# Compression of cached blocks beside dense products: one batch of 64 products a half block in place of two of 32, second layer behind the batch, five turned tiles

## The chip, the core and the metric

One core of a Trainium2 chip runs the whole program. The metric is the device time of one execution in microseconds; the time before is the median of three runs, 1340.01 us (1339.94 to 1341.91). The engines are named as in the profile: PE (TensorE, matmul; PEld its weight loads), DVE (VectorE), ACT (ScalarE), POOL (GpSimd) and SP (SyncE, which here only issues DMAs). Each engine takes its instructions in order; waits between engines go over semaphores.

## The reference

One inference step of a two-layer decoder: 256 prompt tokens and 8 x 4 sample tokens, 288 in all, width 1024. Layer 0 mixes with a gated short convolution, layer 1 with native sparse attention; each has a half-step SwiGLU FFN (2816 wide) before and after it. What the change touches is the compressed branch of the sample rows: blocks of 32 cached rows, gathered over a page table, go through a two-layer MLP into one key and one value.

```python
def compress(rows, pe, w1k, w2k, w1v, w2v):
    B, T = rows.shape[:2]
    blk = rows.reshape(B, T // L_CMP, L_CMP, 2, N_KV_HEADS, HEAD_DIM) + pe[:, None, None, :]
    k = jax.nn.gelu(jnp.einsum('bnlkd,lde->bnke', blk[:, :, :, 0], w1k)) @ w2k
    v = jax.nn.gelu(jnp.einsum('bnlkd,lde->bnke', blk[:, :, :, 1], w1v)) @ w2v
    return k, v
...
past_c = cache_cmp[page_table].reshape(B, past, 2, N_KV_HEADS, HEAD_DIM)
```

The past blocks hang on the cache alone, not on the tokens, so they can be compressed at any time before attention.

## The kernel before

**Dense work.** Weights are streamed by SP into four buffers of 8 KB a partition (`raw`, L96). `Weights.convert` splits each *unit* of at most 8 x 128 x 128 into an exact pair: `whi` by ACT (L116), `wlo` = weight minus `whi` by DVE (L117; a few by POOL). A product (`product`, L177 for every matmul) is three matmuls for each k: hi x hi, hi x lo, lo x hi, all 288 tokens wide. So an up unit of 8 k has 24 matmuls, a down unit of the first half of the hidden values 18 (six k), of the second half 15 (five k). Taking a unit first splits ahead, up to two units beyond the one taken (`AHEAD = 2`).

**Phases.** Three FFNs run with the compression beside them: the first and second around the conv mixer of layer 0, the third ahead of attention. An FFN has for values f0 to f11 two products each (gate, up), then a down phase over d0 to d7 with two units each (a, b), then f12 to f21 and a second down phase. After a pair of products `evacuate` (L484 to L494) takes them over: DVE scales the gate (t), ACT applies Silu (s), DVE scales the other, POOL multiplies (a), and one step later ACT and DVE make the pair Ah, Al of it, the inputs of the down products. In the second down phase each d also updates the residual xT (L523), and `gated` makes from it xh (ACT), xl (DVE), a square (ACT) and adds it up (POOL). At d4 a tiny Sqrt (`root`, L527) brings ACT's table for Sqrt ahead of the norm's own Sqrt (`rms`, L352), which comes after the next phase's first products. Silu and Tanh come from other tables than Sqrt. The conv mixer has 24 products in, three for each d, with gates and taps (L541 to L569), and eight products out.

**Side work.** `cmp_side` (from L713) is a Python generator that the planner resumes: after each unit `tick(cost)` runs what was put off (`later`), then adds cost x FILL (0.13) to what is owed, and steps the generator until the shares it yields have used that up. A tick costs 3.0 in an up phase and in the mixer, 2.2 in a down phase. The place of side work in every engine's queue is therefore fixed by the order of the program.

**Compression.** There are 64 gathered tiles (`load`, L733: a POOL indirect DMA of 512 KB into four slots `rc`). Each is turned by DVE (`turn`, L739) into one of three slots `rt`, and turning tile i starts the gather of tile i + 4. Four tiles make one half block (b, h). Each tile is the moving operand of eight matmuls, which stand as 16 products in the profile (`acc<-rt,W`, two passes each), so a half has 64. Before, they come as two batches of 32 with a pause of 2.0 behind each. `gelu_hidden` (L696 to L699: ACT Hx and its square, DVE, POOL) and `gelu_hidden2` (L703 to L705: Tanh on ACT, DVE, POOL) make the hidden values; `second` (the products `acc<-Hs,W` and `acc<-W,Hs`, then DVE's copy KcT, L791, and ACT's copy Vc, L792) is the second layer, run in the half that follows, behind the pause after its first batch. Ahead of the loop POOL multiplies W1 with the positions (L750) and DVE reduces that (L754) for the bias b1.

Of the kernel before, what the change touches and what calls it, by code (L numbers as in the profile page):

```python
# [10 lines left out]
F32 = mybir.dt.float32  # L11
# [7 lines left out]
P = 128  # L19
D = 1024  # L20
# [17 lines left out]
# buffers: loaded weights, split weights, gathered pages  # L38
RAW, SPLIT, PAGES = 4, 4, 5
ATT = dict(mm=3, tr=3, acc=2)  # L40

# the start: which tile of the input DVE squares, products that warm the array up, steps from a part's
# split to its products, when the tokens' factors are wanted, where weights are split and by which engine
# [4 lines left out]
# the past blocks' compression beside the dense products: its share of the time, and what its loads take  # L48
# [3 lines left out]
# attention: the order of the steps of a round (see nsa), the prompt's items a step, how many of them are  # L52
# kept for the last rounds, where the small steps of a pair of sequences go, which turns ACT takes, and
# where the output projection's weights are split
# [11 lines left out]
class Weights:  # L66
    """The weight stream: chunks of at most 8 KB a partition are loaded ahead, each is split into an
    exact pair of float32r parts, unit by unit, ahead of its products."""
# [76 lines left out]
def tile_step(ctx, tc, x_prompt, x_sample, state_conv, cache_cmp, cache_sel, cache_win, page_table,  # L145
# [33 lines left out]
    # ---- inputs wanted first  # L179
# [3 lines left out]
    xv = [ffn0.tile([P, D], F32, name="rt", bufs=3) for a in range(3)]  # L183
# [24 lines left out]
    # ---- constants  # L208
# [14 lines left out]
    # ---- the stream of weights  # L223
# [78 lines left out]
    # ---- the residual stream, transposed: [d, token]  # L302
# [39 lines left out]
    def gated(d, v):  # L342
        """The normed input's part without the token's factor, as an exact pair; the squares' sum."""
        gated_hi(d, v)
        gated_lo(d, v)
        squares(d)
# [10 lines left out]
    def begin(pg, pu):  # L357
        """The first products, each step as soon as its part of the input has been turned and split."""
        nc.scalar.activation(root, eps, AF.Sqrt)
        r = tmp.tile([P, 4], F32, name="rn")  # L360
        for a in range(3):
            m = min(P, N - a * P)
            sq = ffn0.tile([P, D], F32, name=f"sq{a % 2}", bufs=1)
# [4 lines left out]
        warm = accb()  # L368
# [56 lines left out]
    def products2(p0, p1, ah, al, late=2, between=None):  # L425
        """Two outputs at a phase's start: the inputs that come last are used last."""
# [15 lines left out]
    def tick(cost):  # L442
        """After each unit of dense work: what was put off, and a share of the side work."""
# [165 lines left out]
    # ---- the last norm: turned as it comes, scaled when the tokens' factors are known  # L609
# [45 lines left out]
    # ---- the compressed branch's past blocks: they hang on the cache alone  # L655
# [8 lines left out]
    def indices():  # L664
        # a gathered row is two tokens of a block: partition (q, n) takes tokens 8 q + 2 i of block n
# [47 lines left out]
    def cmp_side(cw):  # L713
# [4 lines left out]
        # rows (q, d) and steps (i, l, h) of a block's token 8 q + 2 i + l and column 32 h + d  # L718
# [17 lines left out]
        def turn(i):  # L736
            if i < 64:
                turned[i] = cw.tile([P, 1024], F32, name="rt", bufs=3)
                nc.vector.transpose(turned[i], tiles.pop(i))  # L739
                load(i + 4)  # L740
# [4 lines left out]
        turn(0)  # L745
        # the first layer's share of the positions: a product with one column
        part = []
        for h in range(2):
            t = cw.tile([P, 1024], F32, name="rt", bufs=3).rearrange("p (s e) -> p s e", s=8)
# [11 lines left out]
        turn(1)  # L761
        second = None
        for b in range(NB):
            for h in range(2):
                H = accb()
                for j in range(4):
                    i = b * 8 + h * 4 + j
                    v = turned.pop(i).rearrange("p (l c k h n) -> p c l h k n", l=2, c=2, k=KV, h=2)
                    turn(i + 2)
                    for st in range(4):  # L770
# [3 lines left out]
                        if st == 3 and j % 2:  # L774
                            yield 2.0
                    if j == 0 and second:
                        gelu_hidden2(*hidden)
                    if j == 1 and second:
                        second()
                        yield 0.6  # L780
# [13 lines left out]
        yield 0.5  # L794
        gelu_hidden2(*hidden)
        yield 1.0
# [734 lines left out]
```

## Time and profile before

| | |
|---|---|
| median of three runs | 1340.01 us |
| span of the profiled execution | 1333.6 us |
| DVE busy, ACT busy, POOL busy | 815.4, 616.7, 353.5 us |
| compression products on PE, first to last | 106.0 to 771.0 us |
| gathers of the compression | 64, median 5.2 us to landing |
| transposes | 64, 78.3 us of DVE |
| granted clock of PE | 0.995 |

The profile shows one execution. Its rows of groups give line, engine, operation, names, shapes and count, then busy time and mean duration in ns, then idle time ahead of them with what ended it. Rows of the timeline give start, duration, engine, line, operation, names and count, and in brackets the idle time ahead and what ended it. Rows of windows give the stretch in us, its length, the busy time of PE with its count, the granted clock, the DMA share and GB/s. Rows of waits give the waiting group, the group that ended the wait, the total, the count and the longest. Matmuls overlap, so a matmul's duration (about 300 ns) is longer than the step from one start to the next (132 ns), and PE counts as busy in gaps shorter than that; starts are what to read.

### The profile page before, as it was taken

What the parts mean: (1) busy time and instruction counts of PE and PEld (TensorE: products, weight loads), DVE (VectorE), ACT (ScalarE), POOL (GpSimd) and SP (SyncE); (2) the same over time, 40 slices, a digit from 0 to 9 for tenths busy, and PEclk for the clock granted to TensorE, in tenths of its full rate; (3) what the DMA queues carried; (4) which work ended last, traced back from release to release, by engine and by line L of the source; (5) the groups of instructions that cost most, each with busy time, mean ns of one, the idle gap of its engine ahead of it and who ended that gap; (6) DMA issues with size and microseconds to landing.
All of it is one profiled execution on the core that took longest, in us unless ns stands there. A gap on an engine that the chain in (4) does not pass through costs nothing.

```text
span 1333.6 us, 26864 instructions
## 1 busy us (share of the span) xinstructions
PE 1309.6 (98%) x11009; PEld 1242.0 (93%) x11009; DVE 815.4 (61%) x1512; ACT 616.7 (46%) x1115; POOL 353.5 (27%) x356
## 2 busy tenths in 40 slices
PE   8999999999999999999999999999999999999997
PEld 8999999999999999999999999998776688999997
DVE  5675566677666555667655555666556456554553
ACT  5443444443454433345433445454766655443444
POOL 2331233243323222333321121303333123220211
PEclk9999999999999999999999999999999998999999
DMA  8767555756565575457656344765577964766432
GB/s 261 197 195 245 187 189 171 234 183 204 191 194 192 162 236 198 144 181 246 193 171 206 127 143 144 215 192 222 206 269 285 300 165 163 246 251 221 142 118 75
DMA packets 202893, 262.12 MB, mean 197 GB/s; under 512 B 14958, under 2 KB 188610, under 8 KB 197524
## 3 DMA queue, kind: packets, MB, share of 16 engines
q1 hardware_dynamic: 179792, 182.34, 43.5%
q0 software_dynamic: 14304, 75.61, 16.0%
q10 hardware_dynamic: 8676, 2.48, 1.0%
q8 instruction: 86, 1.41, 0.4%
q14 instruction: 35, 0.29, 0.1%
HBM read 257.38 MB, written 11.35 MB: 202 GB/s over the span
## 4 chain that ended last, share of the span: by engine, by line
PE 87%; DVE 6%; ACT 4%; issue 2%; POOL 1%; DMA 0%; ACTq 0%; SPq 0%; POOLq 0%; DVEq 0%
PE mm L177 74%; PE acc L177 8%; PE tr L221 4%; DVE wlo L117 2%; ACT whi L116 1%; DVE rt L739 1%; DMA rt<-in_x_prompt_dram 0%; ACT sq L332 0%; ACT wlo L1166 0%; ACT S L1166 0%; DVE xT L523 0%; ACT L527 0%; ACT whi L1280 0%; DVE xl L326 0%; POOL ue L542 0%
## 5 line engine op out<-in xcount | busy, mean ns | idle before, releaser
L177 PE MATMUL mm<-xh,whi 128*128 128x288 f32 x1832 | 548.5, 299 | 2.2 <-DVE xl L1215 0.9
L177 PE MATMUL mm<-xh,wlo 128*128 128x288 f32 x1832 | 544.1, 297 | 2.7 <-DVE wlo L117 1.7
L177 PE MATMUL mm<-xl,whi 128*128 128x288 f32 x1832 | 536.7, 293 | 1.1 <-DVE xl L326 1.1
L117 DVE TENSOR_TENSOR wlo<-raw,whi 128x1024 fp32r<-128x1024 f32 (+2 forms) x358 | 402.2, 1136 | 109.0 <-ACT whi L116 107.2
L116 ACT ACTIVATE whi<-raw 128x1024 fp32r<-128x1024 f32 (+2 forms) x365 | 343.1, 953 | 107.8 <-PE mm L177 90.7
L177 PEld LDWEIGHTS mm<-xh,whi 128*128 128x128 f32 x1832 | 344.8, 188 | 8.1 <-issue 3.9
L177 PEld LDWEIGHTS mm<-xl,whi 128*128 128x128 f32 x1832 | 349.1, 191 | 2.8 <-DVE xl L326 2.5
L177 PEld LDWEIGHTS mm<-xh,wlo 128*128 128x128 f32 x1832 | 344.2, 188 | 3.7 <-DVE wlo L117 2.4
L490 POOL TENSOR_TENSOR a<-s,t 128x288 f32<-128x288 f32 x88 | 111.9, 1271 | 445.8 <-DVE t L488 273.0
L177 PE MATMUL mm<-Ah,whi 128*128 128x288 f32 x768 | 229.4, 299 | 0.0
L177 PE MATMUL mm<-Ah,wlo 128*128 128x288 f32 x768 | 227.9, 297 | 0.7 <-DVE wlo L117 0.7
L177 PE MATMUL mm<-Al,whi 128*128 128x288 f32 x768 | 227.5, 296 | 0.0
L177 PEld LDWEIGHTS mm<-Ah,whi 128*128 128x128 f32 x768 | 145.2, 189 | 2.6 <-issue 1.9
L177 PEld LDWEIGHTS mm<-Ah,wlo 128*128 128x128 f32 x768 | 144.1, 188 | 1.4 <-DVE wlo L117 1.4
L177 PEld LDWEIGHTS mm<-Al,whi 128*128 128x128 f32 x768 | 144.4, 188 | 0.0
L486 ACT ACTIVATE s<-t 128x288 f32<-128x288 f32 x88 | 39.1, 445 | 172.4 <-DVE t L484 170.4
L733 POOL DMA_INDIRECT rc<-in_cache_cmp_kv_dram,idxc x64 | 70.8, 1107 | 134.2 <-DVE rt L739 117.0
L493 ACT ACTIVATE Ah<-a 128x288 fp32r<-128x288 f32 x88 | 39.2, 445 | 128.0 <-POOL a L490 127.7
L488 DVE TENSOR_TENSOR t<-mm,rB 128x288 f32<-128x288 f32 x88 | 39.9, 454 | 79.1 <-PE mm L177 79.1
L739 DVE STREAM_TRANSPOSE rt<-rc 128x1024 f32<-128x1024 f32 x64 | 78.3, 1233 | 9.2 <-PE acc L177 9.1
L494 DVE TENSOR_TENSOR Al<-a,Ah 128x288 fp32r<-128x288 f32 x88 | 40.0, 454 | 58.8 <-ACT Ah L493 58.8
L523 DVE SCALAR_TENSOR_TENSOR xT<-mm,xT 128x288 f32<-128x288 f32 x64 | 29.2, 456 | 71.2 <-PE mm L177 70.9
(348 smaller groups left out, 1249.3 us busy)
## 6 DMA issues: line engine op xcount, KB each, us to landing
raw<-in_w_ffb_gu_dram SPq DMA_DIRECT2D x44, 1024.0 KB
raw<-in_w_ffa_gu_dram SPq DMA_DIRECT2D x42, 1024.0 KB
raw<-in_w_ffa_down_dram SPq DMA_DIRECT2D x16, 768.0 KB
raw<-in_w_conv_in_dram SPq DMA_DIRECT2D x12, 1024.0 KB
raw<-in_w_ffb_down_dram SPq DMA_DIRECT2D x16, 768.0 KB
raw<-in_w_ffa_down_dram SPq DMA_DIRECT2D x16, 640.0 KB
raw<-in_w_ffb_down_dram SPq DMA_DIRECT2D x16, 640.0 KB
out_dram<-in_cache_win_kv_dram POOLq DMA_DIRECT2D x8, 1016.0 KB, 6.9
```

Source lines behind the costliest of these rows:

```text
L116: self.nc.scalar.activation(parts[0], v, AF.Copy)
L117: (lower or self.nc.vector).tensor_sub(parts[1], v, parts[0])
L177: nc.tensor.matmul(out, lhsT, rhs, start=start, stop=stop, skip_group_check=True)
L221: nc.tensor.transpose(out, in_, ident[:k, :k])
L486: nc.scalar.activation(s1, t1, AF.Silu)
L488: nc.vector.tensor_mul(t2, pu[:, :N], rB)
L490: nc.gpsimd.tensor_mul(a, s1, t2)
L493: nc.scalar.activation(Ah[:, f], a, AF.Copy)
L494: nc.vector.tensor_sub(Al[:, f], a, Ah[:, f])
L523: nc.vector.scalar_tensor_tensor(xT[:, d], py[:, :N], 0.5, xT[:, d], op0=OP.mult, op1=OP.add)
L733: nc.gpsimd.indirect_dma_start(out=tiles[i], out_offset=None, in_=rows_c, in_offset=bass.IndirectOffsetOnAxis(ap=idxc[:, i:i + 1], axis=0))
L739: nc.vector.transpose(turned[i], tiles.pop(i))
```

## The change

- A half block's 64 products run as one batch, with no pause inside.
- The second layer of the half before stands right behind the batch; then `gelu_hidden` of this half, still in the same step.
- Then a pause of 2.3, `gelu_hidden2`, and another pause of 2.3. The share of a half is 4.6 as before.
- `rt` has five slots in place of three: three tiles are turned at once at the start and a fourth ahead of the loop, and the tile i + 4 is turned at tile i (before: i + 2).
- The squares of the input at the start of the program (`sq`, L363) use the slots of `rc` in place of two of their own, so the space of the two more `rt` slots comes from there.
- Comments are taken out (left out below).

```diff
-RAW, SPLIT, PAGES = 4, 4, 5
+RAW, SPLIT, PAGES, RT = 4, 4, 5, 5
...
-    xv = [ffn0.tile([P, D], F32, name="rt", bufs=3) for a in range(3)]
+    xv = [ffn0.tile([P, D], F32, name="rt", bufs=RT) for a in range(3)]
...
-            sq = ffn0.tile([P, D], F32, name=f"sq{a % 2}", bufs=1)
+            sq = ffn0.tile([P, D], F32, name="rc", bufs=4)
...
-                turned[i] = cw.tile([P, 1024], F32, name="rt", bufs=3)
+                turned[i] = cw.tile([P, 1024], F32, name="rt", bufs=RT)
...
-        turn(0)
+        for i in range(RT - 2):
+            turn(i)
...
-            t = cw.tile([P, 1024], F32, name="rt", bufs=3).rearrange("p (s e) -> p s e", s=8)
+            t = cw.tile([P, 1024], F32, name="rt", bufs=RT).rearrange("p (s e) -> p s e", s=8)
...
-        turn(1)
+        turn(RT - 2)
...
-                    turn(i + 2)
+                    turn(i + RT - 1)
                     for st in range(4):
                         for c in range(2):
                             mm(H[c * 64:(c + 1) * 64, :P], W1[:, j * 4 + st, c * 64:(c + 1) * 64],
                                v[:, c, st // 2, st % 2], j + st == 0, j + st == 6)
-                        if st == 3 and j % 2:
-                            yield 2.0
-                    if j == 0 and second:
-                        gelu_hidden2(*hidden)
-                    if j == 1 and second:
-                        second()
-                        yield 0.6
+                if second:
+                    second()
                 hidden = gelu_hidden(H, P, cw)
...
-        yield 0.5
-        gelu_hidden2(*hidden)
-        yield 1.0
+                yield 2.3
+                gelu_hidden2(*hidden)
+                yield 2.3
         second()
         yield 0.6
```

## The prediction

> **What bounds the kernel now.** I read the page first: span, busy shares, slices, chain.
>
> ```profile
> span 1333.6 us, 26864 instructions
> PE 1309.6 (98%) x11009; PEld 1242.0 (93%) x11009; DVE 815.4 (61%) x1512; ACT 616.7 (46%) x1115; POOL 353.5 (27%) x356
> PE 87%; DVE 6%; ACT 4%; issue 2%; POOL 1%; DMA 0%; ACTq 0%; SPq 0%; POOLq 0%; DVEq 0%
> ```
>
> TensorE (PE) is the bound, and the chain of waits runs on it for 87%. Next I asked for PE's waits between 100 and 860 us, which holds all of the compression, and for PE's stretches between three insertions of side work, with single rows of its timeline.
>
> ```profile
> PE mm L177 <- DVE wlo L117: 1.7, 4, 0.7
> PE acc L177 <- DVE rt L739: 0.7, 1, 0.7
> ...
> 402.62:404.52 1.90, 1.90 (x34) 1.00 0.05 16
> 404.52:420.57 16.05, 16.05 (x122) 1.00 0.63 198
> 420.57:421.39 0.82, 0.82 (x13) 1.00 0.00 0
> ...
> 402.62 0.55 PE L177 MATMUL acc<-rt,W 128*64 128x128 f32 x6
> 403.98 0.61 PE L177 MATMUL acc<-rt,W 128*64 128x128 f32 x8
> ...
> 407.79 0.30 PE L177 MATMUL mm<-xh,whi 128*128 128x288 f32 x1
> 417.31 0.30 PE L177 MATMUL mm<-xh,whi 128*128 128x288 f32 x1
> ...
> L177 PE MATMUL acc<-rt,W 128*64 128x128 f32 x1024 | 63.2, 276 | 0.7 <-DVE rt L739 0.7
> L177 PE MATMUL acc<-Hs,W 64*64 64x64 f32 x64 | 5.3, 242 | 0.0
> ```
>
> These are PE's two longest waits, 2.4 us in 760, so no stall of size can be removed. What can be removed are **seams**. From 407.79 to 417.31 PE runs three weight units of 24 products, 132 ns each. The stretch of 120 products between a batch and a second layer takes 16.05 instead of 120 x 0.1322 = 15.86: 0.19 too much, though PE counts as busy. Inside a batch, the 12 pairs from 402.62 to 403.98 take 0.113 each, so 16 pairs are 1.81, but the batch takes 1.90: a tail of 0.09. The 1024 batch products at 32 a batch are 32 insertions, the 64 of the second layer at 4 each are 16: 48 in all.
>
> **Seams saved.** After, a half block is one batch of 64 (16 of them), with the second layer of the half before directly behind it, and one second layer stands alone at the end: 17 insertions, 31 stretches fewer, 31 x 0.19 = 5.9 us. Two tails of 0.09 become one, 16 x 0.09 = 1.4. The passage from a batch to a second layer isn't in the trace: between nothing (another 1.3 saved) and a whole seam tail of about 0.2 (1.6 lost over 15); I take a tail, as both are plain float32. Sum **7.3 saved** (5.7 to 8.6).
>
> **Where things fall.** A half costs 4.6 of share before and after; at 0.13 that is 35.4 units of dense cost. The first batch stays in the first down phase (the waits ahead of it are owed at a cost of about 81: 69 by the up phase's ticks, then 2.2 each). From there the ticks give these places for the 16 batches: nine in up phases (three of them between a value's second product and its evacuation: f19 of the first FFN, f11 and f17 of the second), two in 12-row down phases, two in 10-row down phases (d5 of the first FFN, d2 of the second), two inside the conv mixer, one at the conv mixer's last tick; the first is one of the 12-row ones.
>
> ```profile
> 106.01 1.09 PE L177 MATMUL acc<-rt,W 128*64 128x128 f32 x16
> 107.78 1.09 PE L177 MATMUL acc<-rt,W 128*64 128x128 f32 x16 [0.68 <-DVE rt L739]
> 371.02 0.40 PE L177 MATMUL mm<-xh,wlo 128*128 128x288 f32 x1 [0.55 <-DVE wlo L117]
> ```
>
> First batch: its second tile is now late, 1.77 where 8 pairs take 0.90; with four tiles turned ahead this goes, **0.9 saved**. Its fifth transpose will wait for a gather asked for only just before (4.2 to 9.9 us to landing, row below), but two units of split weights cover it: 0 to 0.3 lost. At the second FFN's start PE loses about 0.9 (0.55 of it idle, 371.02) to splits behind the conv state's copies; a batch now stands right before, 4.5 us of cover, but then DVE and ACT are busy with it: **0.6 saved** (0 to 0.9).
>
> **Behind a batch.** The new order puts four transposes, the copy KcT, the copy Vc, Hx and its square in a row ahead of the next split.
>
> ```profile
> 403.42 1.24 DVE L739 STREAM_TRANSPOSE rt<-rc 128x1024 f32<-128x1024 f32 x1
> 106.49 3.49 DVE L739 STREAM_TRANSPOSE rt<-rc 128x1024 f32<-128x1024 f32 x3
> 405.85 1.18 DVE L117 TENSOR_TENSOR wlo<-raw,whi 128x1024 fp32r<-128x1024 f32 x1
> 421.76 0.37 ACT L792 ACTIVATE Vc<-acc 32x256 f32<-32x256 f32 x1 [3.65 <-DVE KcT L791]
> 402.54 0.37 ACT L696 ACTIVATE Hx<-acc,b 128x128 f32<-128x128 f32 x1
> L488 DVE TENSOR_TENSOR t<-mm,rB 128x288 f32<-128x288 f32 x88 | 39.9, 454 | 79.1 <-PE mm L177 79.1
> 404.36 1.04 ACT L116 ACTIVATE whi<-raw 128x1024 fp32r<-128x1024 f32 x1
> ```
>
> Count from the batch's first product. Batch 3.7, second layer 0.8, seam 0.2: PE is back at 4.7, and two units are already split. DVE begins 0.8 in, as at 403.42; four transposes at 1.16 (three take 3.49) end at 5.5, the small copy KcT 5.7; Vc waits for KcT, as its row shows, 6.0; Hx and a square like it 6.7; whi 7.7; wlo 8.9. An up phase wants it after two units, 4.7 + 6.3 = 11.0: 2.1 to spare, nothing lost. Ahead of an evacuation its two operations (0.45 each, by the group) come first: still 1.2. A 12-row down phase has units of 18 products, 2.4, and splits of three quarters: 9.5 against 8.4. A transpose waits for the products of the tile before, at 0.9, 1.8 and 2.7, which is earlier than DVE gets there. What queues behind these waits: on ACT every split's whi, behind Vc; on POOL the products `a`, behind four gathers that each wait for a transpose, which matters only where `a` is wanted at once (f11, below). If this cover were gone, each batch would cost what it is late.
>
> In the **10-row down phases** a unit has 15 products, only 2.0, and the chain of residual, xh and square stands between two splits.
>
> ```profile
> 226.95 0.55 PE L177 MATMUL acc<-rt,W 128*64 128x128 f32 x6
> 228.10 1.23 DVE L739 STREAM_TRANSPOSE rt<-rc 128x1024 f32<-128x1024 f32 x1
> 231.23 0.44 DVE L523 SCALAR_TENSOR_TENSOR xT<-mm,xT 128x288 f32<-128x288 f32 x1
> 575.95 0.78 DVE L117 TENSOR_TENSOR wlo<-raw,whi 128x640 fp32r<-128x640 f32 x1
> 232.59 1.28 ACT L527 ACT_TABLE_LOAD   x1
> 233.89 0.20 ACT L527 ACTIVATE root<-eps 128x1 f32<-128x1 f32 x1
> 235.63 0.40 PE L177 MATMUL mm<-Ah,wlo 128*128 128x288 f32 x1 [0.22 <-DVE wlo L117]
> ```
>
> The batch at 226.95 had its first transpose 1.15 in. Four end at 5.8, and the steps above, with a whi and a wlo of 0.8, give the third unit's split at 8.6 against 4.7 + 4.0 = 8.7. The unit after that waits for residual, xh and square (231.23 to 232.58, where the table load begins: 1.35) and its own split of 1.5, and comes at 11.4 against 10.7; its lower half is wanted only with the third product: **0.5 lost** in the second FFN (0 to 1). In the first FFN the batch stands right behind the load of the root table (1.28 and 0.20), so everything is 1.5 later: 1.1, 0.9 and, at the phase's end, 0.7 late; minus some 0.5 that the load costs PE there now (0.22 of waiting at 235.63 and a seam's worth of starting again): **2.2 lost** (0.5 to 3). And in the second FFN the same table load loses the batch that covers it now: **0.5 lost** (0 to 0.5).
>
> **Second FFN, f11.**
>
> ```profile
> L490 POOL TENSOR_TENSOR a<-s,t 128x288 f32<-128x288 f32 x88 | 111.9, 1271 | 445.8 <-DVE t L488 273.0
> ```
>
> The batch falls between the last product and the evacuation, and `a` must be turned into Ah and Al within 9.1 us: t at 7.3, Silu 7.8, POOL's `a` 1.27 by this row, Ah and Al as long as t: about 10. The last products of the unit can wait a little: **0.7 lost** (0 to 1.5).
>
> **Tanh between two Sqrts.** The Tanh in mid pause of the second FFN's batch at d2 falls at d6 of the same down phase, behind the root table load at d4 and ahead of the norm's Sqrt.
>
> ```profile
> 602.28 1.23 DVE L117 TENSOR_TENSOR wlo<-raw,whi 128x1024 fp32r<-128x1024 f32 x1 [0.77 <-ACT whi L116]
> 603.74 0.29 PE L177 MATMUL mm<-xh,whi 128*128 128x288 f32 x1
> 610.77 0.50 ACT L352 ACTIVATE rms<-acc,eps 128x288 f32<-128x288 f32 x1 [3.57 <-PE acc L177]
> ```
>
> Load 1.28 and Tanh 0.31 (taken as long as an Hx without its bias) come ahead of the split whose lower half ends at 603.5, while PE begins that unit at 603.74 and wants the lower half 0.26 later: **1.1 lost** (0 to 1.6). The load back to Sqrt lies in ACT's 3.57 us of idle time ahead of 610.77. The Trainium skill (ScalarE: Activation LUTs, "What ACT_TABLE_LOAD costs") says to order activations by set and puts a switch at 1283 ns plus 1380 ns of drain; here root begins 0.02 behind a load of 1.28, so the rows decide for the smaller figure. With the page's drain this item would be 2.5.
>
> **Three turns at once, early.**
>
> ```profile
> 79.96 4.59 DVE L117 TENSOR_TENSOR wlo<-raw,whi 128x1024 fp32r<-128x1024 f32 x1 [0.69 <-ACT whi L116]
> 78.95 1.91 POOL L750 TENSOR_TENSOR rt<-W,vecT 128x1024 f32<-128x1024 f32 x1
> 84.96 0.29 PE L177 MATMUL mm<-xh,whi 128*128 128x288 f32 x1
> ```
>
> A split takes 4.59 instead of 1.2 while POOL does the first of two multiplications of the position weights, and ends 0.4 ahead of its product at 84.96. Two more transposes make DVE 2.3 later, but POOL is also put off by its gathers: 0 to 2.3 lost, I take **1.0**.
>
> **Conv mixer.** Its splits stand behind the taps in ACT's queue; two batches make that chain about a microsecond later against a unit of 3.2: **0.7 lost** (0 to 1.8).
>
> **Costed at nothing.** Gathers go four at a time, and each is read a whole half, some 40 us, later.
>
> ```profile
> DMA to landing us min/median/max: 4.2/5.2/9.9
> q0 software_dynamic: 14304, 75.61, 16.0%
> ```
>
> Four are 2.1 MB, 5.9 us of all queues by the second row's share; a weight chunk is wanted six units (12 to 19 us) after its slot falls free, and the two chunks under way are as much again. If that cover went, a late chunk would cost what is left of 5.9. The squares in the gather slots, the end of the side work (still before the third FFN's second down phase) and PSUM banks change nothing.
>
> **Sum.** Saved 7.3 + 0.9 + 0.6 = 8.8; lost 2.2 + 0.5 + 0.5 + 0.7 + 1.1 + 1.0 + 0.7 = 6.7 (with the first batch's 0.1, 6.8). Span 1333.6 - 2.0 = 1331.6. The median of the runs shown, 1340.0, lies 6.4 above this span, and I keep that: **1338.0 us**. With saved and lost half way to their better bounds it is 1334, half way to the worse 1342.
>
> **Rivals.** *All covered:* DVE is idle for 39% of the span, and PE waits for wlo only four times in 760 us now. Then only the 1.0 at the start is lost: 1340.0 - 7.8 = 1332. Against it: the 10-row phases have under 1 us to spare. *Slower, splits late behind every batch:* DVE reaches its first transpose late because it waits in order, for an Al or an evacuation; above 2.1 us more than I took, each batch in an up phase or the mixer costs PE the rest. At 3 us it is 0.9 x 11 = 10 more: 1348. For it: ACT and DVE wait for each other four times in the new order; against it: 403.42. *A second layer is a seam too*, since its products have other tiles: 0.29 x 15 = 4.4 less saved, 1342.4.
>
> **Chances.** Forecast 0.5, all covered 0.2, late everywhere 0.2, second seam 0.1. No change is within 0.2%, 2.7 us. Of the forecast 0.18 is faster, 0.27 the same, 0.05 slower; the second seam is 0.08 and 0.02. So 0.38, 0.35, 0.27. The range takes in the first rival and reaches half way into the second: 1331 to 1346.
>
> **What would show it.** Batches of 3.7 us with 0.8 directly behind, stretches between them of twice the length; the wait at 107.78 gone; waits of PE for wlo in the two 10-row down phases, at f11 and at the third FFN's start, where the Tanh and Sqrt have a table load each. Waits for wlo behind most batches would mean the slower rival; no new ones, the faster.

## The result, and the profile after

| kernel | median | runs | ratio to the kernel before (95% interval) |
|---|---|---|---|
| before, beside the change | 1339.73 us | 6 | |
| changed, first comparison | 1346.95 us (1344.23 to 1349.74) | 6 | 1.0058 (1.0045 to 1.0070) |
| changed, on another chip (e9) | 1336.57 us | 11 | 1.0002 (0.9993 to 1.0011) |
| changed, on a third (e13) | 1336.92 us | 10 | 1.0002 (0.9993 to 1.0012) |
| changed, on a fourth (e17) | 1338.27 us | 10 | 1.0010 (0.9999 to 1.0021) |

The change made the kernel 7.2 us slower in the first comparison, and 0.3, 0.3 and 1.5 us slower on three other chips, where the intervals don't tell it from no change. Both need an explanation: why it isn't faster anywhere, and where 7 us come from in the first comparison.

The page of the changed kernel (first comparison), its span, busy times and chain:

```profile
span 1346.0 us, 26887 instructions
PE 1312.4 (98%) x11009; PEld 1247.2 (93%) x11009; DVE 816.9 (61%) x1512; ACT 618.0 (46%) x1117; POOL 339.6 (25%) x356
PE 79%; DVE 9%; ACT 6%; issue 3%; DMA 1%; POOL 1%; another core or an unknown queue 0%; ACTq 0%; SPq 0%; DVEq 0%; POOLq 0%
```

PE's share of the chain fell from 87% to 79%; DVE's rose from 6% to 9% and ACT's from 4% to 6%. PE's waits of the same kernel between 75 and 860 us (waiting group, what ended the wait, total, times, longest), where the kernel before has 1.7 for wlo, 0.7 for rt and the same 0.6 for the residual xT:

```profile
PE mm L177 <- DVE wlo L117: 7.1, 12, 1.0
PE mm L177 <- ACT whi L116: 2.0, 2, 1.7
PE mm L177 <- ACT Ah L493: 1.7, 1, 1.7
PE mm L177 <- DVE xT L523: 0.6, 1, 0.6
PE mm L177 <- DVE Al L494: 0.3, 1, 0.3
```

Beside splits that are late, there is a wait for `Ah`, the hidden values at f11. The changed kernel's DVE, ACT and PE around that place:

```profile
459.27 0.63 PE L177 MATMUL acc<-W,Hs 64*32 64x64 f32 x8
...
456.51 3.50 DVE L739 STREAM_TRANSPOSE rt<-rc 128x1024 f32<-128x1024 f32 x3 [2.03 <-PE acc L177]
462.26 0.23 DVE L787 COPY KcT<-acc 128x64 f32<-128x64 f32 x1 [2.25 <-remote]
463.79 0.45 DVE L484 TENSOR_TENSOR t<-mm,rB 128x288 f32<-128x288 f32 x1
...
462.52 0.38 ACT L788 ACTIVATE Vc<-acc 32x256 f32<-32x256 f32 x1 [10.19 <-DVE KcT L787]
465.69 0.44 ACT L493 ACTIVATE Ah<-a 128x288 fp32r<-128x288 f32 x1 [0.23 <-POOL a L490]
...
466.18 0.40 PE L177 MATMUL mm<-Ah,whi 128*128 128x288 f32 x1 [1.68 <-ACT Ah L493]
```

The second layer's last product ends at 459.9 and the last transpose at 460.0, so KcT could start there. It starts at 462.26, and the profile has no releaser to name: "remote". Vc waits for KcT, t waits behind it, and PE pays. It is not one place. The changed kernel's view of the KcT copies gives DVE's idle time ahead of them (us, times) by what ended it:

```profile
L787 DVE COPY KcT<-acc x16: 184/225/226, 159.7 to 803.6; 128x64 f32<-128x64 f32 x16
its engine sat idle before it (us, times) until:
  remote: 18.1, 9
  PE acc L177: 5.4, 3
who waited for it (us, times):
  ACT Vc L788: 104.8, 14
```

The trace's records of the semaphore that PE raises (the texts below also call a raise an update) say the same: the raise that belongs to the second layer's last product is recorded 1.0 to 3.2 us after that product's end in eleven of the 16 halves, and in ten of these KcT starts 0.02 behind it. The median over all of PE's raises is 0.014. This became the question of the experiments.

### The profile page after: what moved, and what is told of

It reads as the page before. It is cut to its first block, busy times and chain, and to the rows that moved or that the text cites. A ratio compares the mean times of both kernels' runs of the same rounds, so it can differ in the third digit from the quotient of the medians.

```text
span 1346.0 us, 26887 instructions
## 1 busy us (share of the span) xinstructions
PE 1312.4 (98%) x11009; PEld 1247.2 (93%) x11009; DVE 816.9 (61%) x1512; ACT 618.0 (46%) x1117; POOL 339.6 (25%) x356
## 4 chain that ended last, share of the span: by engine, by line
PE 79%; DVE 9%; ACT 6%; issue 3%; DMA 1%; POOL 1%; another core or an unknown queue 0%; ACTq 0%; SPq 0%; DVEq 0%; POOLq 0%
PE mm L177 68%; PE acc L177 7%; PE tr L221 4%; DVE wlo L117 3%; ACT whi L116 2%; DVE rt L739 1%; DMA raw<-in_cache_sel_kv_dram,idxs 1%; ACT sq L332 0%; DMA rt<-in_x_prompt_dram 0%; ACT wlo L1162 0%; ACT L527 0%; DVE xT L523 0%; ACT S L1162 0%; POOL ue L542 0%
## 5 line engine op out<-in xcount | busy, mean ns | idle before, releaser
L490 POOL TENSOR_TENSOR a<-s,t 128x288 f32<-128x288 f32 x88 | 107.0, 1216 | 414.4 <-DVE t L488 244.2
L733 POOL DMA_INDIRECT rc<-in_cache_cmp_kv_dram,idxc x64 | 64.1, 1002 | 96.5 <-DVE rt L739 82.2
L739 DVE STREAM_TRANSPOSE rt<-rc 128x1024 f32<-128x1024 f32 x64 | 74.7, 1215 | 7.3 <-PE acc L177 5.8
```

The costliest lines, as they stand in the source:

```text
L490: nc.gpsimd.tensor_mul(a, s1, t2)
L733: nc.gpsimd.indirect_dma_start(out=tiles[i], out_offset=None, in_=rows_c, in_offset=bass.IndirectOffsetOnAxis(ap=idxc[:, i:i + 1], axis=0))
```

## The experiments

A stall below is worked out thus: from the first product of a weight unit to that of the next, less 0.1322 a dense product, 0.0566 a batch product and 0.0683 a second-layer product. These are the steps in the rows of the kernel before (407.79 to 417.31; 402.62 to 403.98; the 0.82 of a second layer).

### What holds the second layer's release up

**e1: gathers in the pause.** The gathers that the turns of a batch allow are kept back.

```diff
                 nc.vector.transpose(turned[i], tiles.pop(i))
-                load(i + 4)
+                asked.append(i + 4)
...
                 yield 2.3
                 gelu_hidden2(*hidden)
+                gathers()
                 yield 2.3
```

> The changed kernel, but the four gathers that the four turns of a batch allow are issued together behind the mid-pause's activation, a good 15 us later; batch, second layer, transposes and copies stay where they are. In the changed kernel the update of PE's semaphore by the second layer's last product comes 1.0 to 3.2 us after that product has ended in ten of the halves, all of them with four gathers of 0.94 to 0.98 on POOL around that moment, and within 0.02 in the last three, which have no gathers left; KcT (DVE) waits for it, and ACT's Vc, Hx, square and whi queue behind KcT. Theory A (the gathers' issue holds the update up): KcT starts within 0.3 of the later of the last transpose and the second layer's last product in all halves; the splits behind a batch come about 2 us earlier; of the losses in the conv mixer (about 4.5), at the second FFN's f11 (3.9) and at its start (2.5) about half goes: 1346.9 - 5 = 1342 (1339 to 1344). Rival B (four transposes in a row, or the two tilings of PE one behind the other, hold it up): KcT still starts 1 to 3 us after both, and the time stays at 1346 to 1348.

Measured: 1355.81 us against 1339.59 of the kernel before on the same chip, 1.0118 (1.0101 to 1.0135). KcT came within 0.3 of the later of transposes and second layer in all 16 halves: that half of theory A held. The time did not: the loss moved to POOL. Its rows at the third FFN's start, and PE's:

```profile
615.88 0.97 POOL L737 DMA_INDIRECT rc<-in_cache_cmp_kv_dram,idxc  x1
617.16 0.94 POOL L737 DMA_INDIRECT rc<-in_cache_cmp_kv_dram,idxc  x1 [0.30 <-issue]
618.40 1.05 POOL L737 DMA_INDIRECT rc<-in_cache_cmp_kv_dram,idxc  x1 [0.30 <-issue]
619.75 1.68 POOL L737 DMA_INDIRECT rc<-in_cache_cmp_kv_dram,idxc  x1 [0.30 <-issue]
621.45 2.50 POOL L117 TENSOR_TENSOR wlo<-raw,whi 128x1024 fp32r<-128x1024 f32 x1
...
624.01 0.40 PE L177 MATMUL mm<-xh,wlo 128*128 128x288 f32 x1 [4.16 <-POOL wlo L117]
```

Four gathers in a row keep POOL for 5.5 us here, and a lower half that POOL makes stands behind them: PE waits 4.16. Where gathers are issued is thus a price of its own.

**e4: two transposes (and gathers) in the batch, two in the pause.**

```diff
-                    turn(i + RT - 1)
+                    if j < 2:
+                        turn(i + RT - 1)
...
                 gelu_hidden2(*hidden)
+                turn(i + RT - 2)
+                turn(i + RT - 1)
                 yield 2.3
```

> The changed kernel, but only the first two transposes (and their gathers) stand in the batch; the other two, with theirs, follow behind the mid-pause's activation. DVE is then through with its transposes 3.2 after the batch's first product instead of 5.5, and the second gather's issue ends about where the second layer's last product does. Theory A (gathers' issue holds PE's semaphore update up): KcT starts within 0.5 of the second layer's last product in most halves, wlo comes 2 to 3 us earlier, and in the units after the pause DVE has 2.3 us of cover: 1340 to 1343. Rival B (the two tilings of PE behind one another hold it up): KcT still 1 to 3 us late behind the second layer's end, though DVE and POOL have been done; 1344 to 1347.

Measured: 1343.41 us, 1.0026 (1.0017 to 1.0036), near the 1340 to 1343 of theory A. The raise was late in six halves, by 0.14 to 1.0 us, all of them with the second gather's issue ending within 0.7 of the second layer's end; where it had ended 0.8 or more earlier, or only the first or none had begun (two halves), it was on time.

**e5: the reverse, gathers right ahead of the second layer** in the kernel of e2 (below).

```diff
                 yield 2.0
+                gathers()
                 if second:
                     second()
```

> The reverse test. The kernel with one batch of 64 and the second layer in a step of its own (e2_second_own_step, 1333.9 us) has KcT 0.02 to 0.04 behind the second layer wherever DVE is free, since its gathers are over by then. Here the four gathers are issued directly ahead of the second layer; transposes, batch and the second layer's place stay. Theory A (the gathers' issue holds PE's semaphore update up): with the transposes long done, KcT still comes 1 to 4 us after the second layer's last product in the halves whose gathers stand before it, and Vc behind it. Rival B (the two tilings one behind the other, or four transposes in a row, hold it up): KcT stays within 0.1 wherever DVE is free. The time tells less: the gathers now stand on POOL ahead of other products (`a`, sums of squares) and may cost there, as in e1; 1334 to 1342.

Measured: 1332.44 us, 0.9971 (0.9960 to 0.9982), and no raise late anywhere, though in eight halves gathers were being issued up to the second layer's end or past it. Alone this would refute theory A. But it ran on another chip, and in its profile, and those of e6 to e8 beside it, no raise is late but one, of 0.19 in attention, which every profile has. The profiles of e1 to e4 each have others there too, up to 1.4, though all these kernels share attention. So the chip became the suspect.

**e9, e10, e11: the changed kernel again, with e6 and e7 (below), on one chip.**

> The changed kernel itself, once more, beside e6_activation_late and e7_second_ahead_of_batch on one chip. In the four runs before the last four, and in the changed kernel's first profile, updates of PE's semaphore come 0.2 to 4 us late in 19 to 40 places, some 15 of them in attention, which the change does not touch; in the kernel before and in e5 to e8 there is one such place each, of 0.19. The runs of each group shared a chip. Theory L (late updates belong to the chip or its hour, not to the kernel, and cost where a copy waits for them): if this chip shows none in attention, KcT comes within 0.1 of the later of the last transpose and the second layer's end everywhere, the losses in the mixer, at f11 and at the second FFN's start are smaller by 1 to 2 us each, and the ratio to the kernel before is 1.002 to 1.004 in place of 1.0058; if it does show them, they are back and so is the ratio of about 1.006. Rival K (the order batch, second layer, activations makes them late): KcT is 1 to 3 us late in ten halves whatever attention shows, and the ratio is 1.005 to 1.007.

> e6_activation_late once more, beside the changed kernel on the same chip: the only difference is where Hx and its square stand. Theory L: late updates as many as in the changed kernel beside it (none, or some 20 to 40 with KcT late too). Rival K: none here while the changed kernel has them. In time, if no updates are late: the changed kernel minus 4 to 8 us, which is then the price of the activations' place alone (Hx and square ahead of whi on ACT, Tanh between the Sqrts).

> e7_second_ahead_of_batch once more, beside the other two on the same chip. Its KcT stands ahead of the transposes, so a late update of PE's semaphore would find DVE and ACT with little behind them. Theory L: ratio to the kernel before of 0.994 to 0.997 on either kind of chip, and ahead of e6 by 1 to 3 us without late updates, by more with them.

Measured against 1336.30 of the kernel before: 1336.57, 1.0002 (0.9993 to 1.0011); 1333.02, 0.9967 (0.9955 to 0.9979); 1332.47, 0.9963 (0.9951 to 0.9975). No late raises in any of the three. The change is below the 1.002 to 1.004 that theory L had for such a chip, and e10 gains 3.6 of the 4 to 8 expected. Rival K falls: the same program has ten late halves in one profile and none in another.

**e12 to e18: with the kernel before itself, on two more chips.**

> The kernel before, unchanged, for its profile on the same chip as the next three. Theory L (late updates belong to the chip): if this chip delays, there are 15 or more late updates of PE's semaphore in this profile too, most of them in attention, the stretch from the third FFN's last product to the end takes 499 to 501 us in place of 497, and the time is about 1339 to 1340; KcT, which here stands 15 us behind transposes and gathers, is late by under 0.3. If the chip doesn't delay: none of it, and 1336 to 1337. Rival K (the new order makes them): none in this profile on a chip where the changed kernel has them.

> The changed kernel. Theory L: on a chip that delays, KcT 1 to 3 us late in ten halves and 1.004 to 1.007 of the kernel before; on one that doesn't, KcT on time and 0.999 to 1.002, as on chip 6. Rival K: KcT late though the kernel before shows no late update beside it.

> Activations behind a pause, the second layer behind the batch. On a chip that doesn't delay: 0.9965 to 0.998, as on chips 14 and 6. On one that delays, theory L says that KcT, and behind it Vc and every split of ACT, is late as in the changed kernel, and only Hx and the square are out of the way: 1.000 to 1.004. Rival K says prompt everywhere: 0.9965 to 0.998.

> Second layer ahead of the batch. KcT stands there before the transposes and gathers start, so on either kind of chip it should be on time, and the ratio 0.994 to 0.997. If it is above 0.999 on a chip that delays, something else than KcT pays for the late updates (the transposes, which wait for the batch's products, or attention).

> The kernel before, for its profile. On a chip that delays, theory L: late updates of PE's semaphore in attention (about 15) and a time of 1339 to 1340, the stretch behind the third FFN 499 to 501 us; on one that doesn't, one late update and 1336 to 1337.

> The changed kernel. On a chip that delays: 1.004 to 1.007 of the kernel before, KcT 1 to 3 us late in ten halves; on one that doesn't, 0.999 to 1.001.

> Second layer ahead of the batch. On either kind of chip 0.994 to 0.997, KcT on time.

Measured: the kernel before 1336.67 and 1337.07 (1.0000 and 1.0002 of itself); the change 1.0002 (0.9993 to 1.0012) and 1.0010 (0.9999 to 1.0021); e6 again 0.9980 (0.9967 to 0.9993); e7 again 0.9962 (0.9948 to 0.9976) and 0.9963 (0.9952 to 0.9974). Neither chip had late raises, so what the kernel before and e7 show on one that has them was not seen. KcT in the changed kernel on one of them (e13), in the same view as above:

```profile
L787 DVE COPY KcT<-acc x16: 180/184/225, 156.9 to 797.7; 128x64 f32<-128x64 f32 x16
its engine sat idle before it (us, times) until:
  PE acc L177: 5.0, 2
who waited for it (us, times):
  ACT Vc L788: 99.3, 16
```

And f11 in the same run, in the same rows as above:

```profile
457.37 0.63 PE L177 MATMUL acc<-W,Hs 64*32 64x64 f32 x8
...
454.61 3.50 DVE L739 STREAM_TRANSPOSE rt<-rc 128x1024 f32<-128x1024 f32 x3 [2.03 <-PE acc L177]
458.04 0.23 DVE L787 COPY KcT<-acc 128x64 f32<-128x64 f32 x1
459.57 0.45 DVE L484 TENSOR_TENSOR t<-mm,rB 128x288 f32<-128x288 f32 x1
...
461.48 0.45 ACT L493 ACTIVATE Ah<-a 128x288 fp32r<-128x288 f32 x1 [0.24 <-POOL a L490]
```

Same program, same place: KcT comes 0.04 after the second layer's end at 458.0 instead of 2.36, and Ah 2.3 earlier counted from that end. PE's stall there is 0.3 instead of 3.9.

The two waits of DVE that are left are in the last halves, which have nothing to turn. So two things together make KcT late: a chip whose runs show late raises (the first comparison's and that of e1 to e4, which may be one), and gathers being issued while the second layer ends. On the chip of e1 to e4, e1 and e2 with the gathers elsewhere have no late KcT, e4 with half of them up to 1.0, e3 with all of them 1.8 to 3.2; on four others nothing is late whatever the gathers do. Whether it is the chip or its hour, and what in the gathers does it, stays open.

### What the change costs without late releases

**e2: batch of 64 and five turned tiles alone**, the rest in the order of before.

```diff
                 for j in range(4):
...
+                    if j == 0 and second:
+                        gelu_hidden2(*hidden)
-                if second:
-                    second()
+                yield 2.0
+                if second:
+                    second()
+                    yield 0.6
+                yield 2.0
                 hidden = gelu_hidden(H, P, cw)
...
-                yield 2.3
-                gelu_hidden2(*hidden)
-                yield 2.3
+        yield 0.5
+        gelu_hidden2(*hidden)
+        yield 1.0
         second()
```

> One part of the change alone: one batch of 64 with five turned tiles, but the second layer and the activations in the order of before (Tanh in the next batch, pause of 2.0, second layer, 0.6, pause of 2.0, then Hx and its square). 16 insertions more than the changed kernel: 15 x 0.2 to 0.3 = 3 to 4.5 us more of seams. Theory A (the loss comes from what stands between batch and splits on ACT and DVE: KcT, Vc, Hx, square behind a late semaphore): behind a batch only the four transposes are left (DVE back at 5.5 after the first product), ACT is free at once, so the splits are in time nearly everywhere and most of some 16 us of new stalls goes: about 1347 + 4 - 11 = 1340 (1336 to 1343). Rival C (the four transposes alone make the splits late): stalls stay within 3 us of the changed kernel's and the seams are added: 1348 to 1351.

Measured: 1333.88 us against 1339.59, 0.9959 (0.9945 to 0.9973), 5.7 us faster than the kernel before on a chip with late raises, and 9.5 to 22 faster than e4, e3 and e1 beside it. That is below the 1336 to 1343 of theory A too. Rival C falls: four transposes at once cost next to nothing. The gain of the larger batch is there; the change gives it back with what it moves behind the batch.

**e6: activations behind a pause**, second layer still behind the batch.

```diff
+                yield 1.5
                 hidden = gelu_hidden(H, P, cw)
...
-                yield 2.3
+                yield 1.5
                 gelu_hidden2(*hidden)
-                yield 2.3
+                yield 1.6
```

> The changed kernel with Hx and its square taken from behind the batch to behind a pause of 1.5 (then 1.5, Tanh, 1.6); second layer right behind the batch as in the change. What stands behind a batch on ACT is then only Vc, behind a KcT that is still late. Theory A (KcT and Vc behind the late semaphore are the larger part; Hx and square are 0.7 on ACT): 2 to 4 us better than the changed kernel at most, 1343 to 1346. Rival E (the activations behind the batch are what makes the splits late): nearly all of the stalls go, as in e2, with 15 seams fewer than there: 1330 to 1334.

Measured: 0.9976 (0.9966 to 0.9985), 1333.41 against 1337.10, and 0.9967 and 0.9980 when repeated. Without late raises the place of the activations alone is worth 2.9 to 3.6 us (medians of e9 and e10, e13 and e14). Stalls fall at the end of the first FFN (2.0 to 1.2), at the first of two stalls at the second FFN's start (2.5 to 1.9), in its 10-row phase (1.6 to 0.8) and at the third FFN's start (1.3 to 0.5); the mixer takes 2.8 back (1.2 to 4.0 in e9 and e10), 1.5 of it in products that run at a granted clock of 0.50 in e10 and not in e6 (more of this below). Rival E's number came out, but KcT wasn't late on this chip, so it doesn't decide between the two for a chip where it is.

**e7: the second layer directly ahead of the batch**, activations as in e6.

```diff
+                if second:
+                    second()
                 H = accb()
                 for j in range(4):
...
-                if second:
-                    second()
+                yield 1.5
                 hidden = gelu_hidden(H, P, cw)
```

> As e6_activation_late, but the second layer of the half before stands directly ahead of the batch instead of behind it: the same 16 insertions and the same seams saved as in the change, with KcT and Vc ahead of the transposes and gathers in every queue. Theory A: KcT starts within 0.1 of the second layer's end wherever DVE is free, ACT and DVE owe nothing behind the batch but four transposes, and the stalls of the changed kernel go as in e2_second_own_step; against that kernel 15 seams of 0.2 to 0.3 less: 1333.9 - 4 = 1330 (1328 to 1333). Rival B (the batch and the second layer next to one another are bad in either order) or the four transposes' cost: 1336 or more.

Measured: 1331.30 us against 1337.10, 0.9963 (0.9951 to 0.9976), the same on three more chips (e11, e15, e18): 3.8 to 5.8 us faster than the kernel before, 4.1 to 6.4 faster than the change beside it. It keeps every seam that the change saves. DVE's and ACT's rows of e18 show why it costs so little behind the batch:

```profile
411.42 0.23 DVE L788 COPY KcT<-acc 128x64 f32<-128x64 f32 x1 [0.78 <-PE acc L177]
411.56 4.61 DVE L739 STREAM_TRANSPOSE rt<-rc 128x1024 f32<-128x1024 f32 x4
416.10 1.18 DVE L117 TENSOR_TENSOR wlo<-raw,whi 128x1024 fp32r<-128x1024 f32 x1
...
411.68 0.37 ACT L789 ACTIVATE Vc<-acc 32x256 f32<-32x256 f32 x1 [1.53 <-DVE KcT L788]
411.96 1.04 ACT L116 ACTIVATE whi<-raw 128x1024 fp32r<-128x1024 f32 x1
```

The copies come while the batch runs, whi directly behind Vc, and wlo directly behind the transposes.

**e8: e7 with the first three transposes spread.**

```diff
-        for i in range(RT - 2):
-            turn(i)
+        turn(0)
...
             nc.vector.tensor_reduce(part[h], t.rearrange("p s e -> p e s"), AX.X, OP.add)
+            turn(1 + h)
```

> e7_second_ahead_of_batch with the three transposes at the start not all at once, but one ahead of POOL's first multiplication of the position weights and one behind each of DVE's two sums over them. The changed kernel waits 1.3 us for a split at f11 of the first FFN, the other kernels with three transposes at once 1.8; the kernel before hardly at all. Expected: that wait goes, 1 to 1.8 us less than e7, about 1329. Rival: the wait comes from POOL's multiplication itself (a split of 4.6 us beside it, in the kernel before too) and stays: as e7.

Measured: 1332.25 us, 0.9970 (0.9958 to 0.9981), not better than e7 beside it. The wait at f11 of the first FFN went (stalls of its first up phase 2.3 to 1.2), but 0.5 in its first down phase became 2.4. The cost moved.

**e3: all batches about one unit later.**

```diff
-        yield 0.3
+        yield 0.6
         turn(RT - 2)
```

> The changed kernel with the pause ahead of the loop at 0.6 in place of 0.3, so that most batches fall one unit later: in the second FFN from between f11's second product and its evacuation to behind the first unit of the down phase, from the conv mixer's last unit to behind the second FFN's first value, in the mixer from the second third (d3, d7) to the same part of the values before (d2, d6), and the Tanh in mid pause moves with them. Theory P (the loss is a sum of a few bad places): f11's 3.9 us goes, the second FFN's start loses 2 us less, the 10-row down phases and the up phases stay within 1 us: about 1341 (1338 to 1344). Rival D (every batch pays, wherever it stands): within 2 us of the changed kernel, 1345 to 1349.

Measured: 1349.98 us, 1.0084 (1.0065 to 1.0102). Theory P failed; rival D's 1345 to 1349 is nearer, and a little exceeded. f11's stalls fell from 4.0 to 1.4, but at the second FFN's f1 and f2 came 2.1 and 1.1, in the mixer's products in three of 0.9 to 1.2 (the one of 1.2 stands in the changed kernel too), and 0.4 to 0.8 behind six batches in up phases, where the split now stands behind KcT and, one unit on, the evacuation as well. KcT is 1.8 to 3.2 late in nine halves here.

## Why the prediction was wrong, step by step

Forecast 1338.0 with 1331 to 1346; it came out at 1346.95. The terms, in us of PE time, each as a stall less that of the kernel before (seams taken out where a batch stood there before):

| term | predicted | e13 against e12, one chip | first profile |
|---|---|---|---|
| seams saved | 7.3 | 8.1 | 8.1 |
| first batch | 0.9 saved | 0.9 saved | 0.9 saved |
| second FFN's start | 0.6 saved | **4.9 lost** | **2.6 lost** |
| conv mixer | 0.7 lost | 0.6 lost | **4.7 lost** |
| f11 of the second FFN | 0.7 lost | 0.3 lost | **3.9 lost** |
| first FFN, 10 rows | 2.2 lost | 1.3 lost | 1.3 lost |
| second FFN, 10 rows; root's table | 0.5; 0.5 lost | 0.6; 0.7 lost | 0.8; 0.7 lost |
| Tanh between two Sqrts | 1.1 lost | 1.5 lost | 1.5 lost |
| three turns early | 1.0 lost | 1.3 lost | 1.3 lost |
| sum | -2.0 | +2.2 | +7.8 |

From the second weight unit to the last down product of the third FFN all stalls together grew by 2.1 in e13 against e12 and by 7.8 in the first profile, so no term of size is missing. The first unit is left out: there 14 products of e13 take 0.24 each in place of 0.132, 1.4 us in all, but in e17, the same program, none do.

- **Seams: right, a little small.** A batch of 64 and the second layer behind it run as predicted, and the passage between them costs next to nothing, the better of my two ends: in the rows of e13 below the batch begins at 360.98 and the second layer at 364.63, 3.65 later, where 64 products make 3.62. In the third FFN's up phase two halves cost 1.50 more than their products before and 0.46 after; 0.52 a half, 15 times, and 0.2 at the first batch make 8.1.
- **The step that failed on every chip: "a batch now stands right before, 4.5 us of cover ... 0.6 saved"** at the second FFN's start. The cover is PE's, and PE doesn't need it: the tiles were turned already, so PE ran the batch at once, while DVE reached the first transpose 5.2 late, behind the last residual and xl. Rows of e13:

```profile
360.98 3.71 PE L177 MATMUL acc<-rt,W 128*64 128x128 f32 x64
...
365.75 0.52 DVE L326 SCALAR_TENSOR_TENSOR xl<-xT,vecT,xh 128x288 fp32r<-128x288 f32 x1 [0.60 <-ACT xh L323]
366.18 4.62 DVE L739 STREAM_TRANSPOSE rt<-rc 128x1024 f32<-128x1024 f32 x4
370.72 0.18 DVE L787 COPY KcT<-acc 128x64 f32<-128x64 f32 x1
...
370.94 0.38 ACT L788 ACTIVATE Vc<-acc 32x256 f32<-32x256 f32 x1 [4.90 <-DVE KcT L787]
371.34 0.37 ACT L696 ACTIVATE Hx<-acc,b 128x128 f32<-128x128 f32 x1
373.98 2.00 ACT L116 ACTIVATE whi<-raw 128x1024 fp32r<-128x1024 f32 x2 [0.97 <-ACT rd L605]
...
375.08 0.40 PE L177 MATMUL mm<-xh,whi 128*128 128x288 f32 x1 [1.75 <-ACT whi L116]
376.34 0.61 PE L177 MATMUL mm<-xh,wlo 128*128 128x288 f32 x1 [0.73 <-DVE wlo L117]
```

ACT stands 4.90 us behind Vc, then does Hx, its square, the conv state's copies and their DMAs, and only then the splits. That is the condition of my rival "DVE reaches its first transpose late", which I priced for all batches and not for the one place where it is certain. Two experiments show that this order is the cause. In e7, e11, e15 and e18 the same batch stands at the same place, but KcT and Vc go ahead of the transposes, and the stalls of this start are 0.5, where the kernel before has 1.3; in e4, with two transposes in place of four, they are 1.6. In e6, e10 and e14, where only Hx and its square are out of the way, they are 3.3 to 4.4.

Not all of the loss is waiting. Behind the waits PE ran at half of its clock for a while in some executions. Rows of windows of e13 (stretch, length, busy time of PE with its count, granted clock, DMA share, GB/s):

```profile
368.00:374.00 6.00, 5.33 (x39) 1.00 0.73 231
377.00:382.00 5.00, 5.00 (x22) 0.50 0.92 281
384.00:390.00 6.00, 6.00 (x48) 1.00 0.18 48
```

In e13 23 products step by 0.24 in place of 0.132, 2.5 of the 4.9; in e9 and e17 14 do, 1.5 of the 3.7 lost there; in the first profile none do. So what the order of the queues costs here is 2.2 to 2.6 in all four. In the first profile such a stretch follows the wait at f11 and is 1.5 of its 3.9. The three profiles of the kernel before have none between 30 and 870 us. The prediction had no term for it, and what decides where it falls is not shown.

With 4.9 lost here, and 3.7 in e9 and e17, in place of 0.6 saved, this one step turns -2.0 into +2.3 to +3.5; the other terms give about 1 back, most of it by the seams, and 0.3 to 1.5 was measured on these chips.
- **The step that failed in the first comparison: "the small copy KcT 5.7; Vc waits for KcT, 6.0 ... 2.1 to spare, nothing lost".** The count itself is right: in e13 the third unit's split behind a batch in an up phase ends 1.9 us or more ahead of the product that wants it. Where a late raise holds KcT up by 1 to 3 us, that falls to between 0.1 and 1.5, which still costs PE nothing in up phases; but the mixer and f11, costed with under 2 us to spare, lost 4.7 and 3.9 in place of 0.7 each. The 1348 of the rival came out nearly to the number, but by luck, as another mechanism made it: I took for granted that a copy starts when its products have ended, and nothing in the profile of before shows it otherwise.
- **Base.** I set the span of 1333.6 beside a median of 1340.0 and carried the 6.4 over. This drops out of the forecast change of -2.0 and isn't why it failed, but the 6.4 is no constant. In e12 the same program has a span of 1333.3 in an execution that took 1335.3, so 2.0 of it is span against time. The profile was taken at a granted clock of 0.995 and had one late raise, of 0.19; at that clock the kernel before takes 1335.1 to 1335.3 on average on the four chips without late raises. The median was like those of the chip of e1 to e4, where it takes 1339.6. So the two numbers seem to come from chips of two kinds. That the change takes 1336.6 to 1338.3 on the other chips, close to 1338.0, is luck: the kernel before is faster there too, and the change came out with the other sign.
- **Right:** the root's table uncovered, Tanh between Sqrts (0.4 at the last down unit and 1.1 at the third FFN's start), the second FFN's 10 rows, and the mixer and f11 where releases are on time. The first FFN's 10 rows were taken too dear. An estimate with the drain that the Trainium skill puts beside a table load (ScalarE: Activation LUTs, "What ACT_TABLE_LOAD costs") makes the Tanh item 2.5; the trace doesn't agree, as the stalls measure 1.5, nearer to the 1.1 from the rows, and in e13 the Tanh begins 0.01 behind its load of 1.28.

## What to carry to other kernels

Putting batches together saves their seams, but a larger batch should carry nothing behind it that an in-order engine must wait for: here the second layer and its copies ahead of the batch, and the activations in a step of their own, keep a gain (0.9962 to 0.9963 on four chips) that they give back when they stand behind the batch. When PE doesn't need to wait for a batch's helpers, ask where the helper engine stands at that moment: a batch right after a phase's end finds DVE with the phase's tail still to do, and its work then lands on the next phase's start. A profile and a median need not come from one chip; run both kernels side by side on several before a fraction of a per cent is explained.

## What was not expected of the hardware

- In two of six groups of runs (the first comparison, e1 to e4) raises of PE's semaphore come late: by up to 3.2 us for the second layer's last product while POOL issues gathers, and in attention in two to six places of a profile beyond the one that all profiles have, by 0.2 to 1.4. The records show 14 to 20 late ones in attention, but 10 to 13 of these are gaps: the product's own raise is not recorded, the time is that of the next product's, and in eleven of the twelve of the first profile ACT takes the product over 0.10 to 0.16 after its end. The kernel before takes 1339.6 to 1339.7 beside these and 1336.3 to 1337.1 beside the others, which were on four chips; at one granted clock, 0.993, its averages are 1338.7 on the chip of e1 to e4 and 1336.3 to 1336.7 on the four. The stretch from the third FFN's last down product to the end, the same in all kernels, takes 499.0 to 500.7 us in the five profiles with late raises and 495.5 to 498.1 in the fifteen without, the kernel before's three among these.
- Apart from the program's start and end, the granted clock of PE is 1.00 or 0.50 in these profiles, in stretches of 3.4 or 6.8 us at 0.50 between long ones at 1.00 (e13: 376 to 382 us; e9 and e17: 377 to 381 at the same place; the first profile: none there, but one at 468). One such stretch among dense products costs 1.5 us, and on one chip the kernel before takes 1335.2 at a mean of 0.995 and 1338.3 at 0.991 (the chip of e12).
- Issuing four gathers in a row keeps POOL for 4.7 us (0.98 and three of 0.94, 0.30 between them), and up to 5.5 in e1, where one took 1.68.
